# Sums of the compressed past rows: from VectorE to GpSimd, beside the products

## The chip, the cores and the metric

The kernel runs on one core of one Trainium2 chip. The time is the device time of one launch, in microseconds (us); several runs are made and the median is compared. A core has five engines with queues of their own: TensorE (PE in the profile, its weight loads PEld), VectorE (DVE), ScalarE (ACT), GpSimd (POOL) and SyncE (SP), which here issues nearly all transfers. Each engine works through its instructions in order and waits on semaphores for what others make. A difference of under 0.3%, about 5 us, can't be told from no change here.

## What is computed

One step of a two-layer decoder for two groups of requests: a prompt of 512 tokens and 8 sequences of 4 tokens each (32 columns), with shared weights, at a model width of 1024. Layer 0 is a gated DeltaNet with an FFN, layer 1 a sparse attention with an FFN. The sequences have 256 past rows each in a paged cache; sparse attention wants them compressed to blocks. This is the part of the reference that the change touches: for each group of 16 past rows two weighted sums over its rows, `lo` and `hi`, with weights by position, and their shifted sum.

```
def nsa_context(hist, cmp_pos_w, w_cmp):
    ...
    sub = hist[:, :, :2].reshape(B_, n_sub, CMP_STRIDE, 2, NSA_KV_HEADS, NSA_HEAD_DIM)
    lo = jnp.einsum('bmrckd,crkd->bmckd', sub, cmp_pos_w[:, :CMP_STRIDE])
    hi = jnp.einsum('bmrckd,crkd->bmckd', sub, cmp_pos_w[:, CMP_STRIDE:])
    blocks = lo[:, :-1] + hi[:, 1:]

def swiglu_ffn(h, w_in, w_out):
    gate, up = jnp.split(h @ w_in, 2, axis=-1)
    return (jax.nn.silu(gate) * up) @ w_out
```

The first FFN runs beside it and shares no data with it.

## The kernel before

**Matrix products.** All 544 columns (512 + 32) are held transposed, features in the partitions, in two halves of 256 and 288 columns. A product in full precision is made of three in a faster format: `gemm` (lines 177 to 179) multiplies the high half of a weight tile (`whi`) with the high (`uh`) and the low half (`ul`) of the activations, and its low half (`wlo`) with `uh`. `load_w` brings a tile of 1024 x 128 from memory to `wraw` (three buffers), `split` makes `whi` on ScalarE (line 158) and `wlo` on VectorE (line 159), two buffers each. So a weight tile must go through ScalarE and VectorE before TensorE can use it, and its `wraw` is free for the next load only when `wlo` is made.

**The FFN.** `ffn` runs over 22 column tiles of the hidden layer in two groups of 11. One iteration takes a gate tile (`pg`, in a PSUM bank called `mm`) and an up tile (`pu`, `aux`), for the two halves of the columns in turn: gate, up, gate, up, each 24 matmuls. VectorE scales them by `rstd` (lines 955 and 957, which read PSUM), makes silu with ScalarE's tanh (958, 959) and the low half of the result (961). After each group `proj_add` multiplies with the second weight (line 907 adds to `x`). `rstd` is made ahead of the FFN (lines 196 to 208): column sums on TensorE, a power on GpSimd (line 184), three small steps on VectorE, transposes on TensorE.

**The side work.** While the first FFN runs, `past_blocks` forms `lo` and `hi` for all 8 sequences at once: partition = group of 16 rows, 512 elements of k and v. It has 16 rounds, one for each row r of a group. Round r needs the gathered rows `pg` (an indirect DMA that GpSimd issues, line 1059, three buffers) and two position-weight rows broadcast to all partitions, 256 KB each, which SP loads into buffers of the pool `up`; they bear the names `uh` (for `lo`) and `ul` (for `hi`) there, but have nothing to do with the activations. Loads run two rounds ahead. In round 0 VectorE makes the two products straight into `acc` (`pacc` in the profile, line 1077). From round 1 on GpSimd makes them in place (line 1079) and VectorE adds them to `acc` (line 1080).

**The order.** The program is written as generators: after each FFN iteration `ffn` takes some steps of the side work, 28 in 22 iterations, so that most iterations have one round and some two. A scheduler with a model of the engines then sets the order of the instructions on each engine from this; on the chip each engine keeps to that order. In the profiled execution most rounds stand alone in an iteration (a *plain* round), and rounds 3 and 4, 8 and 9, and 12 and 13 share one (a *double* round).

Of the kernel before, what the change touches and what calls it, by code (L numbers as in the profile page):

```python
# [15 lines left out]
OP = mybir.AluOpType  # L16
# [95 lines left out]
class Net:  # L112
# [935 lines left out]
    def past_blocks(self, out, pb, up):  # L1048


        nc, A, T, V, S, G = self.nc, self.A, self.T, self.V, self.S, self.G
        ident = self.C("ident")
        pw = A["nsa_cmp_pos_w"]
        acc = pb.tile([128, 2, 512], F32, name="pacc", bufs=1)
        got = []

        def load(r):
            g = pb.tile([128, ESPAN], F32, name="pg", bufs=3)[:, 0:512]
            nc.gpsimd.indirect_dma_start(out=g, out_offset=None, in_=self.ckv,
                                         in_offset=bass.IndirectOffsetOnAxis(ap=self.idx_cmp[:, r:r + 1], axis=0))  # L1060
            w = [t.bitcast(F32)[:, 0:512] for t in self.u_tiles(up)]
            for i in range(2):
                self.dma(w[i].rearrange("p (c n) -> p c n", c=2),
                         bass.AP(tensor=pw.tensor, offset=pw.offset + (16 * i + r) * 256,
                                 ap=[[0, 128], [32 * 256, 2], [1, 256]]))
            got.append((g, w))

        for r in range(2):
            load(r)
            yield  # L1070
        for r in range(16):
            if r < 14:
                load(r + 2)
            g, w = got.pop(0)
            for i in range(2):
                if r == 0:
                    V.tensor_tensor(acc[:, i], g, w[i], op=OP.mult)
                else:
                    G.tensor_tensor(w[i], g, w[i], op=OP.mult)
                    V.tensor_tensor(acc[:, i], acc[:, i], w[i], op=OP.add)  # L1080
            yield
        for j in range(4):
            ps = self.aux()
            for i in range(2):
                T.transpose(ps[:, i * 128:(i + 1) * 128], acc[:, i, j * 128:(j + 1) * 128], ident)
            hi = pb.tile([128, ESPAN], F32, name="pg", bufs=3)[:, 0:128]
            S.copy(hi, ps[:, 128:256])
            V.tensor_tensor(out[:, j], ps[:, 0:128].rearrange("p (b m) -> p b m", m=16)[:, :, 0:15],
                            hi.rearrange("p (b m) -> p b m", m=16)[:, :, 1:16], op=OP.add)
# [718 lines left out]
```

## Time and profile before

| | us |
|---|---|
| three runs | 1688.38, 1691.83, 1686.68; median 1688.38 |
| profiled execution | 1684.51 |
| its span, first to last instruction | 1682.7 |
| TensorE busy in the span | 1600.1 |
| VectorE | 1041.9 |
| ScalarE | 710.3 |
| GpSimd | 512.8 |

Busy times are sums over the span; engines run side by side. A row of the timeline gives the start in us from the start of the span, the duration, engine, line, operation, `out<-in` by tile names, the shape, and in brackets the idle time of that engine ahead of it with what ended it. A wait is put down to the instruction whose end came last. "PEclk" is the clock that was granted to TensorE as a share of its full 2.4 GHz. In a table of stretches the numbers are the stretch's length, then the busy time of PE, PEld, DVE, ACT and POOL with the number of instructions, PEclk, the share of time in which the DMA engines were busy, and GB/s.

### The profile page before, as it was taken

Reading aid. Unit: us, or ns where it says so; the run is one execution under the profiler, and the core shown is the slowest. Engines: PE = TensorE matmul, PEld = TensorE weight load, DVE = VectorE, ACT = ScalarE, POOL = GpSimd, SP = SyncE. Lnnn points to the kernel's source line nnn. Section 1 sums busy time; section 2 is a strip of 40 time slices with the busy share of each in tenths; the row PEclk is TensorE's granted clock in tenths of the full one; section 3 lists DMA queues with packets and bytes.
Section 4 is the critical chain, followed back from the end, with each engine's and each line's share of the span. In section 5 each row is a group of like instructions: output and inputs, shape, how many; then the busy total and the mean of one; then the engine's idle time right before and its main releaser. Section 6 shows DMA issues by size and latency. Waiting matters only on the chain.

```text
span 1682.7 us, 32781 instructions
## 1 busy us (share of the span) xinstructions
PE 1600.1 (95%) x12527; PEld 1531.8 (91%) x12527; DVE 1041.9 (62%) x2575; ACT 710.3 (42%) x1796; POOL 512.8 (30%) x829
## 2 busy tenths in 40 slices
PE   8998898998889889999999999999999999999997
PEld 6998788987889789999999999977899999999997
DVE  4878778487555543455456588777965554355543
ACT  5554545553322221223232378778843322223233
POOL 2675546325332310100026376566520000000000
PEclk9999999999989999999999999999999999999999
DMA  6233412268555633535343542434123332333222
GB/s 193 76 78 92 108 36 70 70 172 238 122 134 129 139 88 97 113 119 165 104 133 86 146 101 81 115 125 140 43 76 112 104 105 82 103 97 116 85 87 80
DMA packets 289069, 183.36 MB, mean 109 GB/s; under 512 B 25183, under 2 KB 271784, under 8 KB 288784
## 3 DMA queue, kind: packets, MB, share of 16 engines
q1 hardware_dynamic: 286352, 172.88, 37.5%
q0 software_dynamic: 2560, 8.39, 1.5%
q8 instruction: 98, 1.61, 0.4%
q14 instruction: 59, 0.48, 0.1%
HBM read 159.33 MB, written 26.90 MB: 111 GB/s over the span
## 4 chain that ended last, share of the span: by engine, by line
PE 72%; DVE 10%; DMA 8%; POOL 4%; issue 2%; ACT 2%; SPq 1%; POOLq 0%; DVEq 0%; ACTq 0%
PE mm L179 14%; PE mm L177 14%; PE mm L178 14%; PE aux L177 4%; PE aux L178 4%; PE aux L179 4%; DMA ul<-in_nsa_cmp_pos_w_dram 3%; PE po L1630 2%; DMA uh<-in_nsa_cmp_pos_w_dram 2%; PE aux L1657 2%; DVE hb L595 2%; DVE hb L597 1%; DVE wlo L159 1%; PE mm L1567 1%; SPq L155 1%
## 5 line engine op out<-in xcount | busy, mean ns | idle before, releaser
L179 PE MATMUL mm<-uh,wlo 128*128 128x288 f32 (+2 forms) x1824 | 527.6, 294 | 26.6 <-DVE wlo L159 26.6
L177 PE MATMUL mm<-uh,whi 128*128 128x288 f32 (+2 forms) x1824 | 534.2, 295 | 5.6 <-DVE hb L689 1.7
L178 PE MATMUL mm<-ul,whi 128*128 128x288 f32 (+2 forms) x1824 | 533.3, 293 | 1.6 <-DVE ul L214 1.6
L158 ACT CAST whi<-wraw 128x1024 fp32r<-128x1024 f32 (+5 forms) x231 | 215.9, 935 | 528.2 <-PE mm L178 432.2
L179 PEld LDWEIGHTS mm<-uh,wlo 128*128 128x128 f32 (+1 forms) x1824 | 344.2, 191 | 30.2 <-DVE wlo L159 29.2
L177 PEld LDWEIGHTS mm<-uh,whi 128*128 128x128 f32 (+1 forms) x1824 | 347.3, 191 | 8.8 <-DVE hb L689 2.1
L178 PEld LDWEIGHTS mm<-ul,whi 128*128 128x128 f32 (+1 forms) x1824 | 347.6, 191 | 3.3 <-DVE ul L214 1.8
L159 DVE TENSOR_TENSOR wlo<-wraw,whi 128x1024 fp32r<-128x1024 f32 (+5 forms) x207 | 226.5, 1094 | 96.4 <-ACT whi L158 94.9
L177 PE MATMUL aux<-uh,whi 128*128 128x288 f32 (+1 forms) x704 | 203.2, 289 | 0.0
L178 PE MATMUL aux<-ul,whi 128*128 128x288 f32 (+1 forms) x704 | 202.8, 288 | 0.0
L177 PE MATMUL mm<-hh,whi 128*128 128x256 f32 (+1 forms) x704 | 202.1, 289 | 0.0
L179 PE MATMUL aux<-uh,wlo 128*128 128x288 f32 (+1 forms) x704 | 202.1, 287 | 0.0
L178 PE MATMUL mm<-hl,whi 128*128 128x256 f32 (+1 forms) x704 | 201.4, 288 | 0.0
L179 PE MATMUL mm<-hh,wlo 128*128 128x256 f32 (+1 forms) x704 | 196.5, 288 | 0.0
L178 PEld LDWEIGHTS aux<-ul,whi 128*128 128x128 f32 x704 | 132.7, 189 | 0.0
L177 PEld LDWEIGHTS mm<-hh,whi 128*128 128x128 f32 x704 | 132.6, 188 | 0.0
L178 PEld LDWEIGHTS mm<-hl,whi 128*128 128x128 f32 x704 | 132.6, 188 | 0.0
L177 PEld LDWEIGHTS aux<-uh,whi 128*128 128x128 f32 x704 | 132.4, 188 | 0.2 <-issue 0.2
L179 PEld LDWEIGHTS aux<-uh,wlo 128*128 128x128 f32 x704 | 132.5, 188 | 0.0
L179 PEld LDWEIGHTS mm<-hh,wlo 128*128 128x128 f32 x704 | 129.7, 188 | 0.0
L184 POOL TENSOR_TENSOR ycol<-yvar,nhalf 128x2 f32<-128x2 f32 (+1 forms) x2 | 1.6, 776 | 398.0 <-DVE yvar L1705 398.0
L957 DVE SCALAR_TENSOR_TENSOR fup<-aux,rstd 128x256 f32<-128x256 f32 x88 | 38.6, 439 | 113.0 <-PE aux L179 113.0
(535 smaller groups left out, 2898.3 us busy)
## 6 DMA issues: line engine op xcount, KB each, us to landing
wraw<-in_ffn_w_in_dram SPq DMA_DIRECT2D x88, 512.0 KB
wraw<-in_dn_w_in_dram SPq DMA_DIRECT2D x32, 512.0 KB
wraw<-in_ffn_w_out_dram SPq DMA_DIRECT2D x32, 384.0 KB
wraw<-in_ffn_w_out_dram SPq DMA_DIRECT2D x32, 320.0 KB
hb<-in_state_dn_S_dram SPq DMA_DIRECT2D x32, 256.0 KB
wraw<-in_nsa_w_kv_dram SPq DMA_DIRECT2D x12, 512.0 KB
bskew<-bscr SPq DMA_DIRECT2D x16, 320.0 KB
x<-xd SPq DMA_DIRECT2D x16, 272.0 KB
```

Of the source, the lines that this page charges most:

```text
L155: return self.nc.sync.dma_start(out, in_)
L158: self.S.copy(hi, src)
L159: (self.G if pool_lo else self.V).tensor_tensor(lo, src, hi.bitcast(F32), op=OP.subtract)
L177: self.T.matmul(ps, lhsT=hi[:, k, :], rhs=uh[:, cs], start=first and k == 0, stop=False)
L178: self.T.matmul(ps, lhsT=hi[:, k, :], rhs=ul[:, cs], start=False, stop=False)
L179: self.T.matmul(ps, lhsT=lo[:, k, :], rhs=uh[:, cs], start=False, stop=last and k == kc - 1)
L595: V.tensor_tensor(t, D[a][:, 0:m, l:l + 1].to_broadcast([64, m, n]), row.to_broadcast([64, m, n]), op=OP.mult)
L597: V.tensor_tensor(N[a][:, 0:m, l:32], N[a][:, 0:m, l:32], t, op=OP.subtract)
L957: V.scalar_tensor_tensor(up, pu, 0.5, rstd[:, cs], op0=OP.mult, op1=OP.mult)
L1567: T.matmul(ps, lhsT=QH[:, qs], rhs=mov, start=True, stop=False)
L1630: T.matmul(self.po, lhsT=self.VT[ty][:, kb, g], rhs=m[:, i:i + 2].rearrange("p e q -> p (e q)"), start=False, stop=last and kb > k0 and m ...
L1657: T.transpose(ps[:, i * 128:(i + 1) * 128], P[2 * pr + e][ty][:, a:a + 128], ident)
```

## The change

Products and additions of all 16 rounds are made on GpSimd: those of round 0 go straight into `acc`, in all others the product is made in place and then added. VectorE has no part in the 16 rounds any more; shapes, data and loads stay the same.

```
             g, w = got.pop(0)
             for i in range(2):
-                if r == 0:
-                    V.tensor_tensor(acc[:, i], g, w[i], op=OP.mult)
-                else:
-                    G.tensor_tensor(w[i], g, w[i], op=OP.mult)
-                    V.tensor_tensor(acc[:, i], acc[:, i], w[i], op=OP.add)
+                t = w[i] if r else acc[:, i]
+                G.tensor_tensor(t, g, w[i], op=OP.mult)
+                if r:
+                    G.tensor_tensor(acc[:, i], acc[:, i], t, op=OP.add)
             yield
```

In the changed file all products are line 1077 and all additions line 1079. How the instructions stand now is seen from the built programs. SP's order is the same, row by row. Three places differ in the following way.

GpSimd at rounds 3 and 4 (buffers 6286, 6287 and 6296, 6297), before: four products, then the two gathers for later rounds.

```order
L1079 TENSOR_TENSOR uh_6286<-pg_6284,uh_6286 128x512
L1079 TENSOR_TENSOR ul_6287<-pg_6284,ul_6287 128x512
L1079 TENSOR_TENSOR uh_6296<-pg_6294,uh_6296 128x512
L1079 TENSOR_TENSOR ul_6297<-pg_6294,ul_6297 128x512
L1059 DMA pg_6582<-in_cache_kv_dram,idx_cmp_5203 128x512
L1059 DMA pg_6726<-in_cache_kv_dram,idx_cmp_5203 128x512
```


The same stretch of GpSimd's queue after the change:

```order
L1077 TENSOR_TENSOR uh_6286<-pg_6284,uh_6286 128x512
L1077 TENSOR_TENSOR ul_6287<-pg_6284,ul_6287 128x512
L1079 TENSOR_TENSOR pacc_5861<-pacc_5861,uh_6286 128x512
L1077 TENSOR_TENSOR uh_6296<-pg_6294,uh_6296 128x512
L1077 TENSOR_TENSOR ul_6297<-pg_6294,ul_6297 128x512
L1079 TENSOR_TENSOR pacc_5861<-pacc_5861,ul_6287 128x512
L1059 DMA pg_6582<-in_cache_kv_dram,idx_cmp_5203 128x512
L1079 TENSOR_TENSOR pacc_5861<-pacc_5861,uh_6296 128x512
L1059 DMA pg_6726<-in_cache_kv_dram,idx_cmp_5203 128x512
L1079 TENSOR_TENSOR pacc_5861<-pacc_5861,ul_6297 128x512
```


The additions of each round stand behind its products, those of round 3 partly behind the products of round 4, and each gather behind additions.

VectorE in the same iteration of the FFN, before: three additions stand ahead of line 957 and a fourth ahead of the weight tile's `wlo`.

```order
L958 SCALAR_TENSOR_TENSOR fth_6073<-fth_6073,fa_6072 128x256
L1080 TENSOR_TENSOR pacc_5861<-pacc_5861,uh_6286 128x512
L1080 TENSOR_TENSOR pacc_5861<-pacc_5861,ul_6287 128x512
L1080 TENSOR_TENSOR pacc_5861<-pacc_5861,uh_6296 128x512
L957 SCALAR_TENSOR_TENSOR fup_6074<-aux_6023,rstd_5710 128x256
L959 TENSOR_TENSOR fup_6074<-fth_6073,fup_6074 128x256
L1080 TENSOR_TENSOR pacc_5861<-pacc_5861,ul_6297 128x512
L955 TENSOR_TENSOR fa_6132<-mm_6082,rstd_5710 128x288
L159 TENSOR_TENSOR wlo_6153<-wraw_6150,whi_6152 128x1024
```


The same stretch of VectorE's queue after the change:

```order
L958 SCALAR_TENSOR_TENSOR fth_6073<-fth_6073,fa_6072 128x256
L957 SCALAR_TENSOR_TENSOR fup_6074<-aux_6023,rstd_5710 128x256
L959 TENSOR_TENSOR fup_6074<-fth_6073,fup_6074 128x256
L955 TENSOR_TENSOR fa_6132<-mm_6082,rstd_5710 128x288
L159 TENSOR_TENSOR wlo_6153<-wraw_6150,whi_6152 128x1024
```


The four additions are gone; the rest has kept its order.

GpSimd at the start of the first FFN, from the last operation on the sums of squares (224) to the power for `rstd` (184), before:

```order
L224 TENSOR_TENSOR acc_5277<-acc_5277,sq_5618 128x544
L1079 TENSOR_TENSOR uh_6004<-pg_6002,uh_6004 128x512
L1059 DMA pg_6284<-in_cache_kv_dram,idx_cmp_5203 128x512
L1079 TENSOR_TENSOR ul_6005<-pg_6002,ul_6005 128x512
L1059 DMA pg_6294<-in_cache_kv_dram,idx_cmp_5203 128x512
L184 TENSOR_TENSOR rcol_5701<-var_5700,nhalf_75 128x5
```


The same stretch of GpSimd's queue after the change:

```order
L224 TENSOR_TENSOR acc_5277<-acc_5277,sq_5618 128x544
L1077 TENSOR_TENSOR pacc_5861<-pg_5862,ul_5865 128x512
L1077 TENSOR_TENSOR pacc_5861<-pg_5862,uh_5864 128x512
L1077 TENSOR_TENSOR uh_6004<-pg_6002,uh_6004 128x512
L1077 TENSOR_TENSOR ul_6005<-pg_6002,ul_6005 128x512
L1059 DMA pg_6284<-in_cache_kv_dram,idx_cmp_5203 128x512
L1079 TENSOR_TENSOR pacc_5861<-pacc_5861,uh_6004 128x512
L1079 TENSOR_TENSOR pacc_5861<-pacc_5861,ul_6005 128x512
L1059 DMA pg_6294<-in_cache_kv_dram,idx_cmp_5203 128x512
L184 TENSOR_TENSOR rcol_5701<-var_5700,nhalf_75 128x5
```


Line 184 stood behind two products and two gathers; now it stands behind four products, two additions and two gathers. On TensorE the column sums for `rstd` (line 196) have moved forward by four matmuls there, and the transposes of `rstd` (line 204) stand some 26 matmuls of the FFN later than before.

## Rows read from the trace of the kernel before

**Rows 1.** The page: busy time by engine, and the group of line 179 (busy, mean ns, idle before).
```profile
PE 1600.1 (95%) x12527; PEld 1531.8 (91%) x12527; DVE 1041.9 (62%) x2575; ACT 710.3 (42%) x1796; POOL 512.8 (30%) x829
...
L179 PE MATMUL mm<-uh,wlo 128*128 128x288 f32 (+2 forms) x1824 | 527.6, 294 | 26.6 <-DVE wlo L159 26.6
```

**Rows 2.** Two stretches: length, then busy us (instructions) of PE, PEld, DVE, ACT, POOL, PEclk.
```profile
446.20:621.90 175.70, 150.43 (x1123) 148.19 (x1122) 92.81 (x172) 42.54 (x71) 53.55 (x40) 0.93 0.55 126
1268.10:1408.30 140.20, 140.20 (x1123) 139.97 (x1123) 75.61 (x144) 42.23 (x71) 1.30 (x2) 1.00 0.32 99
```

**Rows 3.** Waits, 430 to 750 us: waiter, releaser: total us, times, longest.
```profile
PE mm L179 <- DVE wlo L159: 24.7, 8, 5.8
...
DVE pacc L1080 <- POOL uh L1079: 43.2, 15, 4.8
...
DVE pacc L1080 <- POOL ul L1079: 25.7, 11, 2.7
```

**Rows 4.** Timeline of VectorE: start, duration, operation, [idle before and releaser].
```profile
522.22 1.22 DVE L159 TENSOR_TENSOR wlo<-wraw,whi 128x1024 fp32r<-128x1024 f32 x1
...
534.44 0.69 DVE L1080 TENSOR_TENSOR pacc<-pacc,ul 128x512 f32<-128x512 f32 x1 [2.24 <-POOL ul L1079]
...
536.21 1.22 DVE L159 TENSOR_TENSOR wlo<-wraw,whi 128x1024 fp32r<-128x1024 f32 x1
```

**Rows 5.** Timeline of TensorE, where it restarts behind a wait for wlo.
```profile
495.32 0.58 PE L179 MATMUL mm<-uh,wlo 128*128 128x256 f32 x1 [5.25 <-DVE wlo L159]
...
537.48 0.39 PE L179 MATMUL mm<-uh,wlo 128*128 128x256 f32 x1 [1.73 <-DVE wlo L159]
...
555.51 0.58 PE L179 MATMUL mm<-uh,wlo 128*128 128x256 f32 x1 [5.76 <-DVE wlo L159]
...
601.65 0.58 PE L179 MATMUL mm<-uh,wlo 128*128 128x256 f32 x1 [5.41 <-DVE wlo L159]
...
685.03 0.39 PE L179 MATMUL mm<-uh,wlo 128*128 128x256 f32 x1 [2.90 <-DVE wlo L159]
```

**Rows 6.** Stretches right behind the first and the last of those; PEclk is third from the end.
```profile
494.20:501.00 6.80, 5.68 (x26) 5.68 (x27) 4.52 (x8) 1.90 (x4) 1.76 (x1) 0.50 0.75 197
685.30:688.70 3.40, 3.40 (x18) 3.40 (x18) 1.50 (x3) 0.00 (x0) 0.00 (x0) 0.51 0.67 196
```

**Rows 7.** Timeline of GpSimd: a sum of line 224, products of a plain and a double round.
```profile
435.84 1.78 POOL L224 TENSOR_TENSOR acc<-acc,sq 128x544 f32<-128x544 f32 x1 [4.21 <-ACT sq L223]
...
530.17 1.31 POOL L1079 TENSOR_TENSOR uh<-pg,uh 128x512 f32<-128x512 f32 x1 [8.16 <-DMA uh<-in_nsa_cmp_pos_w_dram]
...
533.10 1.31 POOL L1079 TENSOR_TENSOR ul<-pg,ul 128x512 f32<-128x512 f32 x1 [1.62 <-DMA ul<-in_nsa_cmp_pos_w_dram]
...
549.64 1.26 POOL L1079 TENSOR_TENSOR uh<-pg,uh 128x512 f32<-128x512 f32 x1 [1.70 <-DMA uh<-in_nsa_cmp_pos_w_dram]
```

**Rows 8.** Timelines of GpSimd and VectorE where both want two operands from SBUF.
```profile
966.96 2.66 POOL L1547 TENSOR_TENSOR QL<-qf,QH 64x512 fp32r<-64x512 f32 x2
...
968.82 1.87 DVE L159 TENSOR_TENSOR wlo<-wraw,whi 128x1024 fp32r<-128x1024 f32 x1 [0.37 <-ACT whi L158]
...
969.69 2.76 POOL L165 TENSOR_TENSOR wraw<-wraw,nv 128x1024 f32<-128x1024 f32 x1
```

**Rows 9.** Timeline of VectorE, one iteration of the second FFN.
```profile
1363.92 1.23 DVE L159 TENSOR_TENSOR wlo<-wraw,whi 128x1024 fp32r<-128x1024 f32 x1 [0.54 <-ACT whi L158]
...
1366.10 0.46 DVE L957 SCALAR_TENSOR_TENSOR fup<-aux,rstd 128x288 f32<-128x288 f32 x1 [0.25 <-PE aux L179]
...
1367.10 1.23 DVE L159 TENSOR_TENSOR wlo<-wraw,whi 128x1024 fp32r<-128x1024 f32 x1
```

**Rows 10.** Start of the first FFN: GpSimd, and TensorE's transposes of rstd.
```profile
457.27 1.30 POOL L1079 TENSOR_TENSOR ul<-pg,ul 128x512 f32<-128x512 f32 x1
...
460.17 1.45 POOL L184 TENSOR_TENSOR rcol<-var,nhalf 128x5 f32<-128x5 f32 x1
...
462.27 0.24 PE L204 MATMUL aux<-ct,rcol 32*128 32x32 f32 x1 [1.87 <-DVE rcol L187]
```


## The prediction

> **What bounds the kernel now.** I read the page first: TensorE is busy 95% of the span, so only what makes TensorE wait, or run at a low clock, can move the time [rows 1]. Its one large wait on another engine is for wlo, the low half of a weight tile that VectorE makes in line 159: 26.6 us [rows 1].
>
> Next I set two stretches of equal work side by side. From the last addition to x before the first FFN to the first one behind its first 11 column tiles, TensorE executes 1123 matmuls in 175.70 us; the same stretch of the second FFN, which has no side work on the past rows, has the same 1123 in 140.20 us and never idles [rows 2]. So the side work costs the first FFN 35.5 us here: 175.70 - 150.43 = 25.3 us of idle TensorE, and about 10 us of low clock (0.93 against 1.00).
>
> The waits say whose fault it is. VectorE waits 43.2 + 25.7 = 68.9 us for GpSimd's products, in the sum of line 1080, and TensorE 24.7 us in eight waits for wlo [rows 3]. VectorE runs in order: wlo stands behind the sum, the sum behind the product, the product behind the load of the position weights. In a plain round VectorE waits 2.24 us for the product of ul, makes the sum at 534.44, the queued lines 957, 959 and 955 behind it, and wlo only at 536.21 [rows 4]; TensorE restarts at 537.48 after 1.73 us [rows 5]. Where two rounds fall into one FFN iteration the wait is 5.25, 5.76 and 5.41 us, and there is a late one of 2.90; the other four of the eight, that of 1.73 among them, are together 24.7 - 19.3 = 5.4 us [rows 5]. After the wait of 5.25 us the granted clock is 0.50 (the 1.2 GHz level) for 6.8 us, which costs 3.4; after the 2.90 it is 0.51 for 3.4 us, which costs 1.7 [rows 6].
>
> **The change part by part.** VectorE loses 2 products and 30 sums of 0.69 us, and with them the wait for GpSimd. GpSimd gains 32 operations. Its product of this 128x512 shape takes 1.26 to 1.31 us, its sum of 128x544 in line 224 takes 1.78 us with a wait in it [rows 7]; these bound a sum of 128x512, which the trace doesn't have on GpSimd, and 1.30 is taken, since the product has the same operands and size. The order of the SP queue is unchanged, so the loads of the position weights and of the weights keep their places.
>
> If nothing else happened, the whole 35.5 us would go. But the two engines exclude each other. At 968.82 VectorE's wlo starts while GpSimd makes QL (966.96 to 969.62); it takes 1.87 instead of 1.23 us and ends 1.07 behind GpSimd. GpSimd's next operation starts at 969.69 and takes 2.76, ending 1.76 behind wlo [rows 8]. So each ran only when the other was through: wlo waits out one GpSimd operation, and then has its turn. I apply this to the operations with two operands in SBUF, wlo and lines 958, 959 and 961; lines 955 and 957 read PSUM and are counted as free (if they weren't, two more turns would come in, up to 2.6 us a round, which is the case *slower* below). Before, VectorE was mostly parked during the products; now four operations a round meet its running work. This is the price, worked out per round, with the end of the gate tile's wlo as 0.
>
> *A plain round.* The second FFN gives the undisturbed beat: wlo of the gate tile at 1363.92, line 957 at 1366.10 (released by TensorE, 0.25 idle), wlo of the up tile at 1367.10 [rows 9]. A matmul takes 140.20 / 1123 = 0.125 us on the mean of 256 and 288 columns [rows 2], 0.117 at 256, and an iteration of 96 takes 12.0. The gate tile's wlo ends at 1365.15 and is wanted at the third matmul of the next iteration, which starts at 1366.0: some 1366.25, so it has 1.1 us to spare. The up tile's ends at 1368.33 and is wanted when the gate tile's 24 matmuls are through, 2.8 us on, about 1369.1: 0.75 us. The products start, as before, at +6.7 and +9.7 (530.17 and 533.10 [rows 7] against a gate wlo that ends at 523.44 [rows 4]). The first delays only line 959, which has time. The second, 9.7 to 11.0, and the two sums stand among gate wlo (due 10.8), 961, 958, 959 and up wlo, in turns: gate wlo 11.0 to 12.2, sum to 13.5, 961 to 13.9, sum to 15.2, 958, 957 and 959 to 16.3, up wlo to 17.5 against 12.0 + 3.95 = 15.95. A wait of 1.5 us; once TensorE is late by that, the next train meets it later and less, so 1.2 on average. Five such rounds cost 6; the four short waits before cost 5.4. Bill: **-1 us**.
>
> *A double round.* The third product starts at +12.2 (549.64 [rows 7] against 537.43 [rows 4]), the first two as in a plain round, the fourth 2 to 3 us behind the third; eight operations in all. VectorE has five of its own between gate and up wlo, so at most five of GpSimd's can get in ahead: 6.5 less the 2.2 us of spare time (0.75, the 1.1, and some 0.35 of idle VectorE) gives 4.3 at most. Taken in turns as above, up wlo ends at 19.4 against 15.95: a wait of 3.4 us, and by the row of 2.90 another 1.7 for the clock, 5.1 together. Before it was 5.5 on the mean + 3.4 = 8.9. Three of them: **+11.4 us**.
>
> *The late round* before 685 cost 2.90 + 1.7 = 4.6 us [rows 5, 6], again with wlo queued behind both sums; in the new order no sum is ahead of it. Less 1 for the last round's meetings: **+3.6**.
>
> *The start.* GpSimd's power of line 184, on which rstd and every eviction of the FFN rest, now stands behind four products, a gather and two sums. It ran at 460.17; the product of ul had started at 457.27, as its load landed [rows 10], and the 1.6 us between them are a gather. So it comes at 457.3 + 1.3 + 1.6 + 2.6 + 1.6 = 464.4, 4.2 us later. TensorE has 26 more matmuls, 3.2 us, ahead of the transposes now. Its wait there was 1.87 us [rows 10]; it becomes 1.87 + 4.2 - 3.2 = 2.9, and up to 5 since TensorE gets there sooner when VectorE doesn't wait for the first loads. Bill: **-1** (0 to -3, with the clock).
>
> GpSimd itself has room: per round 4 x 1.3 + 1.6 for the gather = 6.8 us, and 28 / 22 = 1.27 rounds fall into an iteration of 12.0. Only the transposes that follow the last round wait for its last sum.
>
> Sum: -1 + 11.4 + 3.6 - 1 = 13 us. The profiled execution (1684.51 us, span 1682.7) would become 1671.5; it lies 3.9 us under the median of 1688.38, to which I add the same 13: **1675.4 us**. A difference of under 0.3%, about 5 us, can't be told from no change.
>
> **The rivals.** *Cover*: the sums meet VectorE in its idle time and no wait is left. For it: VectorE is busy only 75.61 of 140.20 us in the second FFN [rows 2]. Against it: the second product lands right at the gate wlo. It gives the 35.5 us but 3 for the start, and 3.6: 36 us, 1652 us.
>
> *Swap*: meetings take the place of the wait, and nothing is won; it needs the double rounds to stay at 8.9 us, that is, the eight operations to cost their bound of 4.3 and a second wait in the next iteration, where their last two sums run into the gate wlo. Then only the late round's 3.6 is left against 2 for plain rounds and start: 1687 us. The Trainium skill speaks for this one (Perfetto Trace Analysis, Optimizing Scalar/DVE Operations): the two engines share an SBUF read port, so offloading between them might not help. By that rule alone the sum would be zero; the rows agree on the port, but they also show that the old wait was longer than the port's.
>
> [...]
>
> **How the numbers follow.** The forecast, a gain of 6 to 25 us, has 0.60; cover 0.10, swap 0.18, slower 0.12. Faster by over 0.3%: 0.60 + 0.10 = 0.70; within: 0.18; slower: 0.12. The likeliest case runs from 1663 to 1682; with swap and a little of both ends the range is 1659 to 1691.
>
> **What would show it.** Right: VectorE's idle time on GpSimd is gone; wlo and lines 958, 959, 961 of the first FFN show rows of 1.5 to 2.5 us; TensorE's waits there move from the gate tile (mm) to the up tile (aux), 1 to 4 us long, with a sum of 12 to 18 against 25.3; the stretch of 175.7 us falls to about 166. Wrong: waits of over 5 us that stay; a stretch of about 140 us (cover); a low clock in every iteration (slower); a wait at the transposes of rstd of over 5 us.

## The result, and the profile after

The changed kernel takes **1664.19 us** (median of four runs, 1659.93 to 1667.08) against 1688.69 for the kernel before, run beside it: ratio 0.985, 95% interval 0.984 to 0.987. That is 24.5 us faster, 1.5%. The forecast was 1675.4, with a range of 1659 to 1691: the direction and the range hold, the gain is about twice the 13 us that the sum gave. The profiled execution took 1664.61 us, its span is 1662.4. Medians leave out one execution each of the experiments e6 (8234 us) and e8 (3104 us).

The page of the changed kernel: busy time by engine, and the group of line 179.

```profile
PE 1596.2 (96%) x12527; PEld 1526.5 (92%) x12527; DVE 1059.6 (64%) x2543; ACT 710.8 (43%) x1796; POOL 562.3 (34%) x861
...
L179 PE MATMUL mm<-uh,wlo 128*128 128x288 f32 (+2 forms) x1824 | 524.0, 292 | 4.8 <-DVE wlo L159 4.8
```

TensorE's idle time behind wlo has gone from 26.6 us [rows 1] to 4.8. VectorE executes 32 instructions fewer and is yet *busier* by 17.7 us. That is the price of the port, and below it is seen row by row.

Stretches of the changed kernel: length, then busy us (instructions) of PE, PEld, DVE, ACT, POOL, PEclk, DMA share, GB/s. The first is the stretch of [rows 2] in the first FFN, the last the same in the second FFN.

```profile
447.33:602.00 154.67, 145.13 (x1123) 143.91 (x1122) 108.90 (x143) 42.74 (x71) 95.46 (x68) 0.97 0.63 143
...
466.63:473.46 6.83, 5.07 (x23) 5.01 (x24) 5.90 (x11) 1.45 (x3) 5.42 (x5) 0.50 0.59 171
...
602.00:802.30 200.30, 200.30 (x1598) 199.25 (x1597) 99.44 (x170) 52.77 (x86) 12.36 (x8) 1.00 0.43 120
...
1247.80:1387.90 140.10, 140.10 (x1123) 139.87 (x1123) 75.57 (x143) 42.20 (x71) 1.30 (x2) 1.00 0.33 98
```

Before, the first was 175.70 us [rows 2], and the one that follows it, which holds the late round, was this:

```profile
621.90:827.00 205.10, 202.20 (x1598) 200.78 (x1597) 97.23 (x174) 52.92 (x86) 5.17 (x4) 0.99 0.43 117
```

So 21.0 + 4.8 = 25.8 us were won here; the rest of the program, which the change doesn't touch, took 5.5 us more in this execution, and the medians say 24.5. Of the 35.5 us that the side work cost in the first stretch 14.5 are left. They are accounted for: 154.67 - 145.13 = 9.5 us in which TensorE stands, and the time at the lower clock, 6.8 us behind the start (0.50 in the second stretch above) and 3.4 us behind the wait of 2.20, half of which is lost, 5.1.

Waits of the changed kernel, 430 to 750 us: waiter, releaser: total us, times, longest.

```profile
DVE rs_w L185 <- POOL rcol L184: 7.2, 1, 7.2
...
PE aux L204 <- DVE rcol L187: 5.6, 1, 5.6
...
PE mm L179 <- DVE wlo L159: 2.9, 2, 2.2
...
PE aux L179 <- DVE wlo L159: 0.9, 1, 0.9
```

The 68.9 us in which VectorE stood in the sum [rows 3] are gone: the view has no row in which VectorE waits at `pacc`. In place of TensorE's eight waits for wlo there are three. The longest wait is now another one: the transposes of rstd (line 204).

**A plain round.** VectorE, GpSimd and TensorE in one plain round, and VectorE in the second FFN for comparison (start, duration, operation).

```profile
517.66 1.23 DVE L159 TENSOR_TENSOR wlo<-wraw,whi 128x1024 fp32r<-128x1024 f32 x1 [0.54 <-ACT whi L158]
518.80 1.52 DVE L961 TENSOR_TENSOR hl<-fup,hh 128x256 fp32r<-128x256 f32 x1
520.25 1.54 DVE L958 SCALAR_TENSOR_TENSOR fth<-fth,fa 128x288 f32<-128x288 f32 x1
521.71 0.45 DVE L957 SCALAR_TENSOR_TENSOR fup<-aux,rstd 128x288 f32<-128x288 f32 x1
522.19 1.07 DVE L959 TENSOR_TENSOR fup<-fth,fup 128x288 f32<-128x288 f32 x1
523.18 1.21 DVE L159 TENSOR_TENSOR wlo<-wraw,whi 128x1024 fp32r<-128x1024 f32 x1
...
1343.60 1.23 DVE L159 TENSOR_TENSOR wlo<-wraw,whi 128x1024 fp32r<-128x1024 f32 x1 [0.54 <-ACT whi L158]
...
1345.08 0.45 DVE L958 SCALAR_TENSOR_TENSOR fth<-fth,fa 128x288 f32<-128x288 f32 x1
...
1346.78 1.23 DVE L159 TENSOR_TENSOR wlo<-wraw,whi 128x1024 fp32r<-128x1024 f32 x1
```

```profile
518.30 1.74 POOL L1077 TENSOR_TENSOR ul<-pg,ul 128x512 f32<-128x512 f32 x1 [2.20 <-DMA ul<-in_nsa_cmp_pos_w_dram]
520.00 1.47 POOL L1079 TENSOR_TENSOR pacc<-pacc,uh 128x512 f32<-128x512 f32 x1
521.43 1.51 POOL L1079 TENSOR_TENSOR pacc<-pacc,ul 128x512 f32<-128x512 f32 x1
```

```profile
524.71 0.28 PE L179 MATMUL aux<-uh,wlo 128*128 128x256 f32 x1
...
1350.63 0.28 PE L179 MATMUL aux<-uh,wlo 128*128 128x256 f32 x1
```

The two engines take turns: lines 961, 958 and 959 have grown from some 0.45 us to 1.52, 1.54 and 1.07, each behind one operation of GpSimd, while line 957, which reads PSUM, keeps its 0.45. From the end of the gate tile's wlo to that of the up tile's it is 5.50 us (518.89 to 524.39) where the second FFN needs 3.18 (1344.83 to 1348.01). But the last fence shows when TensorE wants the up tile's wlo: at 1350.63, 2.62 us after it is made. Here it is 0.32 us after. The delay of 2.32 us is paid out of time that was to spare. This is the longest of the plain rounds: the four others between 525 and 590 us need 4.7 to 4.9.

**The longest wait left.** VectorE, GpSimd and TensorE in the double round of 8 and 9.

```profile
554.31 4.18 DVE L159 TENSOR_TENSOR wlo<-wraw,whi 128x1024 fp32r<-128x1024 f32 x1
```

```profile
553.88 0.97 POOL L1059 DMA_INDIRECT pg<-in_cache_kv_dram,idx_cmp  x1 [0.16 <-POOL pacc L1079]
554.88 1.30 POOL L1079 TENSOR_TENSOR pacc<-pacc,ul 128x512 f32<-128x512 f32 x1
556.13 1.26 POOL L1077 TENSOR_TENSOR uh<-pg,uh 128x512 f32<-128x512 f32 x1
558.22 1.41 POOL L1077 TENSOR_TENSOR ul<-pg,ul 128x512 f32<-128x512 f32 x1 [0.83 <-DMA ul<-in_nsa_cmp_pos_w_dram]
```

```profile
558.54 0.39 PE L179 MATMUL mm<-uh,wlo 128*128 128x256 f32 x1 [2.20 <-DVE wlo L159]
```

No turns here: VectorE's wlo comes up at 554.31, waits out the gather, a sum *and* a product, and gets through only when GpSimd pauses at 557.39. That was not in the forecast, and the experiments follow it up.

### The profile page after: what moved, and what is told of

It is laid out like the page before. It is cut to its first block, busy times and chain, and to the rows that moved or that the text cites. A ratio compares the mean times of both kernels' runs of the same rounds, so it can differ in the third digit from the quotient of the medians.

```text
span 1662.4 us, 32746 instructions
## 1 busy us (share of the span) xinstructions
PE 1596.2 (96%) x12527; PEld 1526.5 (92%) x12527; DVE 1059.6 (64%) x2543; ACT 710.8 (43%) x1796; POOL 562.3 (34%) x861
## 4 chain that ended last, share of the span: by engine, by line
PE 76%; DVE 10%; POOL 4%; DMA 4%; ACT 3%; issue 3%; SPq 1%; POOLq 0%; DVEq 0%; ACTq 0%
PE mm L179 15%; PE mm L177 15%; PE mm L178 15%; PE aux L177 5%; PE aux L179 5%; PE aux L178 5%; PE po L1629 2%; PE aux L1656 2%; DVE hb L595 2%; DVE hb L597 1%; SPq L155 1%; DVE wlo L159 1%; PE mm L1566 1%; PE mm L818 1%; PE mm L1567 1%
## 5 line engine op out<-in xcount | busy, mean ns | idle before, releaser
L159 DVE TENSOR_TENSOR wlo<-wraw,whi 128x1024 fp32r<-128x1024 f32 (+5 forms) x207 | 233.1, 1126 | 108.6 <-ACT whi L158 107.1
```

The source lines that it names most:

```text
L159: (self.G if pool_lo else self.V).tensor_tensor(lo, src, hi.bitcast(F32), op=OP.subtract)
```

## The experiments

In what follows the stretch is always the one of 154.67 us above, found by the same two additions to x; idle is its length less TensorE's busy time in it, clock is half the time at the lower level. All twelve experiments stand in this table. The time is a median, the last three columns are of the one profiled execution; the ratio is to the kernel before, run beside each.

| run | us | ratio to before | stretch | idle | clock |
|---|---|---|---|---|---|
| before | 1688.7 | 1 | 175.7 | 25.3 | 11.9 |
| the change | 1664.2 | 0.985 | 154.7 | 9.5 | 5.1 |
| e1 power first | 1659.0 | 0.981 | 156.3 | 10.4 | 5.1 |
| e2 no arithmetic | 1647.1 | 0.975 | 140.1 | 0 | 0 |
| e3 one more sum | 1675.8 | 0.993 | 168.0 | 19.0 | 8.5 |
| e4 all on VectorE | 1689.0 | 1.001 | 175.2 | 22.6 | 15.4 |
| e5 no double rounds | 1657.4 | 0.982 | 146.1 | 3.4 | 1.7 |
| e6 e1 and e5 | 1658.5 | 0.981 | 150.7 | 6.9 | 3.4 |
| e7 gather between | 1678.5 | 0.994 | 171.1 | 23.0 | 8.5 |
| e8 sums later | 1654.5 | 0.981 | 143.6 | 1.5 | 1.7 |
| e9 only the sums | 1665.7 | 0.987 | 152.9 | 9.5 | 1.7 |
| e10 e8, round 0 later | 1659.1 | 0.984 | 147.9 | 5.9 | 3.4 |
| e11 e10 and e5 | 1656.7 | 0.982 | 147.8 | 5.0 | 3.4 |
| e12 e11 and power first | 1647.3 | 0.977 | 140.1 | 0 | 0 |

**What is there to win.** e2 keeps one round's products and leaves out the rest of the arithmetic:

```
-                t = w[i] if r else acc[:, i]
-                G.tensor_tensor(t, g, w[i], op=OP.mult)
-                if r:
-                    G.tensor_tensor(acc[:, i], acc[:, i], t, op=OP.add)
+                if r == 15:
+                    G.tensor_tensor(acc[:, i], g, w[i], op=OP.mult)
```

> The changed kernel with the products and additions of rounds 0 to 14 left out (round 15 keeps its two products); the gathers, the loads of the position weights and their buffers stay. It gives what the arithmetic on GpSimd still costs in the changed kernel. Theory 'spare time': the stretch of the first FFN that takes 140.2 us in the second one and 154.7 in the changed kernel falls to 140 to 142, since all of its 14.5 us are waits behind GpSimd (5.8 at the start, 4.3 for wlo) and the low clock they leave (5.1): 1649 to 1652. Rival 'transfers': part of the cost is that the position weights and the FFN's weights share the DMA engines; then the stretch stays at 146 or more, and the time at 1655 or more.

Its stretch is that of the second FFN, with the DMA engines busy at 0.60 instead of 0.33:

```profile
444.95:585.07 140.12, 140.12 (x1123) 139.88 (x1122) 75.58 (x143) 42.09 (x71) 1.20 (x1) 1.00 0.60 134
```

So the loads cost nothing here; all that the side work costs is its arithmetic, and the bound is 1647.1 us, 2 us below the range that was expected.

**Is it the place in line, or GpSimd?** e4 puts all products and sums on VectorE; e8 leaves them where they were before, but queues a round's sums one round later.

```
-                    V.tensor_tensor(acc[:, i], acc[:, i], w[i], op=OP.add)
+            if r:
+                due.append(w)
+            while len(due) > (r < 15):
+                w = due.pop(0)
+                with self.tc.issue_after(self.hl.ins):
+                    for i in range(2):
+                        V.tensor_tensor(acc[:, i], acc[:, i], w[i], op=OP.add)
```

> All products and additions of all rounds on VectorE, at the places that the scheduler gives them; GpSimd keeps the gathers alone. No meeting at the port is left. Theory 'wait in line': what cost the time before is that wlo stands in VectorE's order behind an operation that waits for a load; it still does, only the product in between is shorter (0.69 instead of 1.3 us), so VectorE's waits are now for the transfers of the position weights, some 40 to 60 us of them, and TensorE's waits for wlo stay within 30% of the 24.7 us of the kernel before: 1678 to 1692. Rival 'slow products': the 1.3 us of GpSimd's product were what made the wait; then most of the 24.7 us go and the time is 1660 to 1670.

> The kernel before, with VectorE's sums of round r queued one round later, behind the last VectorE operation of the FFN iteration in which round r + 1 is issued; products stay on GpSimd, sums on VectorE, so nothing is moved between engines. Theory 'wait in line': the products are done long before their sums come up, VectorE's 68.9 us of waits for GpSimd go, TensorE's waits for wlo fall from 24.7 to under 5 us, with fewer meetings at the port than in the changed kernel (two operations of GpSimd a round, not four): 1652 to 1660. Rival 'load on VectorE': it is the work taken off VectorE that brings the gain of the changed kernel; then this one stays above 1670.

e4 takes 1689.0 us, no different from before. The waits of e4, 430 to 750 us:

```profile
DVE uh L1077 <- DMA uh<-in_nsa_cmp_pos_w_dram: 39.1, 13, 4.4
...
DVE ul L1077 <- DMA ul<-in_nsa_cmp_pos_w_dram: 22.8, 13, 2.6
...
PE mm L179 <- DVE wlo L159: 21.2, 7, 6.7
```

VectorE waits 61.9 us for the transfers where it waited 68.9 for the products [rows 3], and TensorE's waits for wlo are 22.2 us (21.2, and 1.0 at the up tile) where they were 24.7: GpSimd's slower product was not the cause. e8 moves no work between engines and is some 10 us faster than the change. Its stretch:

```profile
443.71:587.28 143.57, 142.05 (x1123) 141.45 (x1122) 101.62 (x165) 42.01 (x71) 55.22 (x40) 0.99 0.67 153
```

So it is the wait in line ahead of wlo that cost the time, and moving the sums to GpSimd is one way among others of taking it away.

**What a meeting costs.** e3 gives GpSimd one more sum in each of rounds 1 to 15.

```
+                    if i and r:
+                        G.tensor_tensor(t, g, t, op=OP.add)
```

> The changed kernel with one more GpSimd addition of the same shape and operands in each of rounds 1 to 15, behind the round's second sum (into a buffer that is not read again, so the output is the same). Theory 'spare time': the up tile's wlo has about 2.6 us of spare time, each of GpSimd's operations that meets VectorE takes 1.1 to 1.3 of it, and the plain rounds of the changed kernel use nearly all of it without a wait; one more operation puts each plain round about 0.5 to 1 us over and each double round 1.3 more: 6 x 0.7 + 3 x 1.3, some 8 us of new waits for wlo, the most of them at the up tile, and 0 to 5 of clock: 1670 to 1678. Rival 'meetings are free': VectorE's queue takes longer operations without TensorE noticing, since the wait in line was the whole cost: within 2 us of the changed kernel, 1662 to 1667.

1675.75 us is the forecast's number, but the trace shows it for another reason. In the plain rounds from 525 to 562 us the trace has no wait of TensorE. The added sum does meet VectorE there (the gate tile's wlo takes 2.19 us at 535.21, where 1.23 is its time alone), but the spare time just covers it: this wlo is ready 0.30 us before TensorE uses it, the up tile's 0.05. The time went where GpSimd's train, that is, its operations without idle time between them, starts behind a gather: four operations of VectorE there are held up by 3.7 to 5.3 us each, a fifth by 1.8, and TensorE's waits for wlo, 3.8 us in the changed kernel, are 13 (and 6.1 at the start, where the wait stands at wlo instead of the transposes). So in plain rounds a meeting costs nothing, as the rival said, but only as long as there is time to spare.

**The gather.** In the traces I then set every VectorE operation with two operands in SBUF that took over 1.3 us longer than alone beside GpSimd's queue. In the stretch there are 4 in the changed kernel, 5 in e1 and 5 in e3, and in all of them the operations of GpSimd that went first had started right behind a gather. All others were held up by 1.2 us at most. e7 puts the gather of each round between its products and its sums; e5 gives each round an iteration of its own.

```
-                        for _ in range((j + 1) * steps // 22 - j * steps // 22):
+                        for _ in range(([2] + [1] * 16 + [2] * 5)[j] if steps == 28 else ...):
```

> The changed kernel with each round's gather put between its products and its two sums, so that in every plain round the sums start right behind a gather; the number of operations is the same. Theory 'gather': in plain rounds VectorE's operation that comes up during the gather is held up until both sums are through, 2.6 to 3.6 us at once where it was 1.1 at most; up wlo comes 0.5 to 1 us later than with turns and TensorE waits a little in several plain rounds: 1666 to 1676. Rival 'chance': the long hold-ups have nothing to do with the gather; in plain rounds turns of 1.1 us stay, and the time is that of the changed kernel, 1661 to 1667.

> The changed kernel with the 28 steps of side work spread in another way over the 22 iterations: 2 in the first, one in each of the next 16, 2 in each of the last 5, so that each round has an iteration to itself. In the traces of the changed kernel and of the two runs above, VectorE's operation and GpSimd's take turns in trains that begin behind a wait for a transfer (no VectorE operation is held up by more than 1.1 us), but where a product or sum starts right behind a gather, as happens only in double rounds, VectorE is held up until GpSimd pauses: 2.3 to 6.7 us in 5 places. Theory 'gather': without double rounds no VectorE operation of the first FFN is held up by more than 1.2 us, TensorE's waits for wlo (3.8 us in the changed kernel) fall under 1 us and the clock behind the longest of them stays up; the wait at the start (5.6 + 3.4) stays: 1655 to 1660. Rival 'amount': waits come from the number of meetings, which is the same, and are only spread over more iterations: 1662 to 1667.

A plain round of e7, VectorE and GpSimd:

```profile
525.02 0.41 DVE L961 TENSOR_TENSOR hl<-fup,hh 128x256 fp32r<-128x256 f32 x1
525.36 3.49 DVE L958 SCALAR_TENSOR_TENSOR fth<-fth,fa 128x288 f32<-128x288 f32 x1
```

```profile
524.17 1.79 POOL L1060 DMA_INDIRECT pg<-in_cache_kv_dram,idx_cmp  x1 [0.15 <-issue]
525.98 1.30 POOL L1089 TENSOR_TENSOR pacc<-pacc,uh 128x512 f32<-128x512 f32 x1
527.23 1.29 POOL L1089 TENSOR_TENSOR pacc<-pacc,ul 128x512 f32<-128x512 f32 x1
```

Line 958 waits out both sums, 3.04 us more than alone (0.45 at 1345.08 above), where the same round of the changed kernel had turns of 1.1. Eleven such rows stand in e7, and it takes 1678.5 us, 14 more than the changed kernel and 2.5 above what I had expected. e5 does the opposite and comes out in its range, the four runs within 1 us, though not as forecast in all: the wait at the transposes, which was to stay at 5.6 us, is 3.2. From its third iteration on nothing is held up by over 1.3 us and TensorE has no wait for wlo of over 0.5 us; two operations, held up by 3.9 and 4.9 us, again in trains behind a gather, stand at the start, where the first rounds still run close together.

**The start.** e1 queues the power for rstd ahead of the products of rounds 0 to 2, e9 gives the two products of round 0 back to VectorE, e6 is e1 and e5 in one.

```
+                with nullcontext() if r > 2 else self.tc.issue_after(self.pw.ins):
                     G.tensor_tensor(t, g, w[i], op=OP.mult)
```

> The changed kernel with GpSimd's power for rstd (line 184) queued ahead of the products of rounds 0 to 2; all else as it was. In the changed kernel var is ready at 453.9 us of the span, but the power starts only at 465.5, TensorE waits 5.6 us at the transposes of rstd and its clock is at the lower level for 6.8 us behind that. Theory 'queue': the place in GpSimd's queue is the whole of it; the power starts at about 455, the wait at the transposes is under 1 us, the low clock behind it is gone: 5.6 + 3.4 = 9 us faster, about 1655; the rounds pushed back by some 5 us are not missed. Rival 'shifted': the two rounds that now run later meet the first FFN iterations, and a wait for wlo of 2 to 5 us comes in there: 1658 to 1664. Rival 'no cover': the power waits for something else and TensorE still waits over 3 us there: 1662 to 1665.

> The changed kernel with the two products of round 0 back on VectorE: one part of the change undone, the 30 sums stay on GpSimd. It sizes the term of the start. By the order of GpSimd's queue the power for rstd then stands behind two products fewer, 2.6 us earlier, and TensorE's wait at the transposes falls from 5.6 to about 3 us with 3.4 us less or more of clock; but VectorE waits in line for the first position weights again, which made TensorE wait 1.8 us for ul of the FFN's activations in the kernel before. Theory 'queue': net gain 1 to 4 us, 1660 to 1663. Rival: the two exchange one for the other, 1663 to 1667, no difference that can be told.

> Both of these: the power for rstd ahead of the products of rounds 0 to 2, and no double rounds. If the start, the double rounds and the clock behind them are all that is left (the run without the arithmetic has 1647.1), it comes within 5 us of that run: 1647 to 1652. By the rival 'amount' the rounds pushed behind the power meet the FFN in other places and waits for wlo of 5 us or more are left: 1656 to 1662.

In e1 the wait at the transposes falls from 5.6 to 0.3 us, as the theory said. But the profiled execution (1666.1, the slowest of four that go down to 1652.4) has a wait for wlo of 5.7 us in its place, at the first double round: the rival "shifted", and the place is again behind a gather, with wlo held up by 6.6 us. The median, 1659.0, lies in that rival's range, and its interval (0.978 to 0.984) meets that of the change (0.984 to 0.987), so a gain is not certain. In e9 the wait at the transposes falls to 3.9 us, where about 3 was expected, but one of 1.4 us for ul comes back, and the double rounds are as they were: 1665.7, no different from the changed kernel, as its rival said. e6 missed its range. What it shows is the same thing at the start, where the rounds that were pushed back run as one train:

```profile
469.59 8.15 DVE L961 TENSOR_TENSOR hl<-fup,hh 128x288 fp32r<-128x288 f32 x1
```

```profile
468.83 1.08 POOL L1059 DMA_INDIRECT pg<-in_cache_kv_dram,idx_cmp  x1 [0.30 <-issue]
469.92 1.31 POOL L1080 TENSOR_TENSOR pacc<-pacc,uh 128x512 f32<-128x512 f32 x1
...
476.17 1.25 POOL L1080 TENSOR_TENSOR pacc<-pacc,ul 128x512 f32<-128x512 f32 x1
477.58 1.03 POOL L1059 DMA_INDIRECT pg<-in_cache_kv_dram,idx_cmp  x1 [0.16 <-issue]
```

An operation of 0.45 us takes 8.15: six operations of GpSimd go ahead of it. TensorE waits 4.9 us behind that, and the 5.6 us won at the start are spent.

**A version that beats both.** With the sums on VectorE, one round later, GpSimd's trains are two products long. e10 takes round 0's products out of the line at the start as well, e11 removes the double rounds, e12 puts the power first.

> The run with VectorE's sums one round later, and in addition the two products of round 0 (on VectorE) queued behind the FFN iteration in which round 0 is issued, instead of ahead of the FFN. In that run TensorE waited 1.3 us for ul of the activations behind these products and ran 3.4 us at the lower clock behind the wait, 3 us in all; with the products out of the line both go: 1650 to 1654 against its 1652.7 to 1657.2. If instead the column sums or the power now end last at the start, the wait moves to the transposes and nothing is gained: 1653 to 1657.

> The run just above with, in addition, no double rounds (2 steps of side work in the first iteration, one in each of the next 16, 2 in each of the last 5). With both, no VectorE operation should be held up by more than 1.2 us and TensorE should have no wait of over 1 us in the first FFN; the run without any arithmetic has 1647.1 and is the bound: 1647 to 1652. Rival: double rounds cost nothing once sums are out of the line, since only two of GpSimd's operations a round meet VectorE: the same as the run above within 2 us.

> The run just above (sums on VectorE one round later, round 0 out of the start, no double rounds) with GpSimd's power for rstd queued ahead of the products of rounds 1 and 2. There TensorE still waited 5.0 us at the transposes of rstd, since the power stands behind four products and a gather and starts at 461.7 us; with the power first it starts at about 453 to 455, that wait and the 3.4 us of clock behind it go, and the stretch of 147.8 us falls to 140 to 143: 1648 to 1652, within 5 us of the run without arithmetic. Rival: products 1 and 2, now late, hold up VectorE behind a gather at the first iterations, as in the earlier run with the power first: a wait of about 5 us comes back there and the time stays at 1654 to 1658.

e10 missed: without the wait for ul TensorE reaches the transposes sooner, 11 us into the stretch, while the power, still behind two products and their loads, starts 15.4 us into it (13.7 in e8), and a wait of 5.9 us stands there, the rival's case, and 2 us more than the rival gave. e11 missed for the same reason (5.0 us), though its body is clean. e12 has **1647.27 us** (1644.28 to 1651.80, five runs), ratio 0.977 (0.9745 to 0.9789): 40 us faster than before, where the change has 24.5, at the bound of e2, and 0.7 us below the range that was expected. Its stretch, and the power in GpSimd's timeline:

```profile
444.11:584.24 140.13, 140.13 (x1123) 139.90 (x1122) 97.57 (x161) 42.15 (x71) 49.35 (x35) 1.00 0.63 148
```

```profile
450.79 1.20 POOL L184 TENSOR_TENSOR rcol<-var,nhalf 128x5 f32<-128x5 f32 x1 [9.24 <-DVE var L201]
```

TensorE doesn't stand at all in the stretch. All arithmetic is done and none of it is seen.

## Why the prediction was right, and where its sizes were off

- **What bounds the kernel: right.** The wait in VectorE's line ahead of wlo was the cost; e4 and e8 show it from both sides, and e2 that all 35.5 us were the arithmetic's.
- **Plain and double rounds: the term that was mis-sized.** Idle and low clock together were 32.0 us before (21.8 + 10.2), the forecast left 21.3 of them (6 + 15.3), and 5.5 are left (3.8 + 1.7). The working of the meetings comes near: from gate wlo to up wlo I had 5.3 us, and the plain rounds take 4.7 to 5.50. Part of that is luck, since in the round shown the product of ul came behind the gate tile's wlo and held up line 961, where I had it ahead of that wlo. What failed is one sentence: that the up tile's wlo "is wanted when the gate tile's 24 matmuls are through, 2.8 us on, about 1369.1: 0.75 us". I worked that out from the code's order of products. TensorE's own rows say 2.62 us to spare, since the second half of the gate tile's columns is started ahead of it. With 1.87 more to spare a plain round's wait of 1.5 is none, and a double round's 3.4 is 1.5, under the 2.2 that the worst of them shows. The trace of before has it too: the up tile's wlo that ends at 1368.33 is first used 2.62 us later.

```profile
1370.95 0.28 PE L179 MATMUL aux<-uh,wlo 128*128 128x256 f32 x1
```

- **Double rounds: wrong in kind.** I had turns throughout. In three of the four long rows two operations of GpSimd went ahead of VectorE's one, behind a gather. The three double rounds waited 0.92 + 0.72, 2.20 and nothing, 3.8 us in all; with the spare time put right the turns would give 3 x 1.5 = 4.5. That these two come near each other is luck, since what held VectorE up was another thing.
- **The late round: right.** 3.6 expected, 4.8 measured (205.10 to 200.30).
- **The start: right place, too cheap.** The power was to come at 464.4 in the time of before, which is 465.5 here (the stretch begins 1.1 us later); it came at 465.47 (GpSimd's row of line 184 in the trace of the changed kernel). The wait was put at 2.9, up to 5, and is 5.64, since VectorE no longer waits for the first loads and TensorE comes sooner, which I had as the upper end. And the lower clock behind it lasts 6.83 us where it was 3.41 before. Before, the start cost 1.87 [rows 10], 1.6 for ul and 1.7 of clock, 5.2 us; now it costs 5.64 + 3.4 = 9.0. So it is 4 us worse, not 1. "A wait at the transposes of rstd of over 5 us" was named as a sign of error, and it stands there.
- **The rivals.** Cover (1652) is closer to the mechanism than I gave it credit for: in plain rounds no wait is left, though the sums do meet VectorE's operations. Swap fell, though its reason is real: VectorE is 17.7 us busier for the port. The Trainium skill (Perfetto Trace Analysis, Optimizing Scalar/DVE Operations) warns that work moved between the two engines might not help for that reason. The trace agrees on the port and not on the outcome, since the time that VectorE lost was to spare. The case of a slower kernel fell too: TensorE has no wait in a plain round.

- **The signs.** Gone are VectorE's waits for GpSimd, and lines 961 and 958 show rows of 1.5 us, as I had said. But the waits did not move to the up tile: 2.9 of the 3.8 us for wlo are still at the gate tile. TensorE's idle time in the stretch is 9.5 us, not 12 to 18, and the stretch is 154.7 us, not 166.

Put together: 26.5 from the rounds, some -4 from the start and 4.8 from the late round are 27, against the 25.8 won in the two stretches that the change touches.

## What to carry to other kernels

Read when a consumer first *uses* a buffer from its own row, not from the order of the source: the spare time between that row and the end of the producer decides whether a slower producer costs anything. Where an engine works in order, a wait ahead of an urgent operation delays that one too (here 68.9 us of VectorE's waits were behind 24.7 us of TensorE's); queue the dependent work one round later, behind the urgent one, before moving it to another engine. And when work is moved, look at what stands in the new queue behind it: one small operation on which the next stage rests (here a power of 1.2 us) can cost more than all the meetings: 9.0 us at the start against 5.5 in the rounds.

## What the chip showed that I had not expected

- GpSimd and VectorE take turns in trains that don't start behind a gather: no VectorE operation with two operands in SBUF is held up by over 1.2 us there. The Trainium skill (SBUF — State Buffer, Who interferes with whom) gives the port as an exclusive lock and says that a VectorE instruction with two SBUF inputs contends for it with a GpSimd instruction that reads SBUF; the traces agree, and line 957 with one of its operands in PSUM never grew (0.46 us at most).
- Every longer hold-up stands in a train that starts right behind an indirect gather in GpSimd's queue: VectorE was held up until GpSimd paused, by 1.5 to 7.7 us, in 4 rows of the changed kernel, 5 of e1, 5 of e3, 2 of e5, 2 of e6, 11 of e7 and 4 of e9. That it goes with the gather's place is shown by e7, which made it happen in plain rounds, and by e5, which took it away there; what in the engine does it stays open. The gather is not enough by itself: in one plain round of e7 a wlo was under way as the train began behind the gather, and turns were taken.

```profile
580.97 1.62 POOL L1089 TENSOR_TENSOR pacc<-pacc,uh 128x512 f32<-128x512 f32 x1
```

```profile
580.22 1.23 DVE L159 TENSOR_TENSOR wlo<-wraw,whi 128x1024 fp32r<-128x1024 f32 x1 [0.82 <-ACT whi L158]
581.36 1.51 DVE L961 TENSOR_TENSOR hl<-fup,hh 128x256 fp32r<-128x256 f32 x1
582.80 1.55 DVE L958 SCALAR_TENSOR_TENSOR fth<-fth,fa 128x288 f32<-128x288 f32 x1
```

- A gather is 1.0 us in GpSimd's timeline, and 1.8 where a wlo was under way as it began (524.17 in e7, the wlo from 523.57); beside a wlo that began just behind it, it kept its 1.0 (523.09 and 523.18 in the changed kernel).
